# A hybrid transformer layer on one core: TensorE pinned to the source's order, first up weights split sooner, convolution steps at a later rank

## The chip, the cores and the metric

The kernel runs on one core of a Trainium2 chip. TensorE does the matrix products, VectorE (DVE), ScalarE (ACT) and GpSimd (POOL) work on rows, and SyncE (SP) issues most of the transfers. The metric is the device time of one execution in microseconds; lower is better.

## The reference

One layer over 2048 tokens of width 1024, in float32: a gated linear attention (GLA) mixer with a residual, a feed-forward network with a causal convolution of three taps and a residual, and a last normalization. Cut to what is computed:

```
h = rmsnorm(x, mix_norm_w)
q, k, v, r, glr = split(h @ w_in)                 # 512, 512, 1024, 1024, 16 columns
log_a = log_sigmoid(glr @ w_gate2 + b_gate) / 16   # one gate per token, head and key
g = cumsum(log_a within chunks of 64 tokens)
k_dec = k * exp(g_end - g)
for each chunk:                                    # 4 heads, keys of 128, values of 256
    state = state * exp(g_end) + k_dec.T @ v
    o = q @ state
x = x + (rms_normalize(o) * norm_w * silu(r)) @ w_out
h = rmsnorm(x, ffn_norm_w)
u = h @ w_up                                       # 1024 -> 5632
u = u[t] * cw[2] + b + u[t-2] * cw[0] + u[t-1] * cw[1]
gate, val = split(u)                               # 2816 each
x = x + (silu(gate) * val) @ w_down
out = rmsnorm(x, final_norm_w)
```

## The kernel before

**Products.** Each float32 product is three matmuls on halves: a value is split into a rounded part hi (a cast on ScalarE) and the rest lo (a subtraction on VectorE, `split`), and `mm3p` (L179 to L189) issues hi·lo, lo·hi, hi·hi (lines L184, L185, L186 of the profile). The large products are cut further into 2 x 2 blocks and computed as seven block products p1 to p7 on sums and differences of the blocks; one such block product with 512 columns is 4 x 3 = 12 matmuls.

**Stages.** First come passes over the rows of x: R (the gate r and the gates' rank-16 projection), A and B (k, q, v of two heads each, with the chunk scan laid between their products), then Y (out-projection). After R the gates are finished: for each tile of 128 tokens `sums` makes pd on TensorE (L639) and an Exp on ScalarE (L640), and `totals` transposes its result into pe (L631). In the scan, og (L763) is a normalized and gated row of outputs, which TensorE transposes into px (L771). In Y a finished row of x goes to `x1_done`: sum of squares on ScalarE (L224), variance on VectorE (L226), its root on GpSimd (L228), the scaled row on ScalarE (L831); `blocks` then transposes it (pt_d, L840).

The up stage (`phase_u`) runs a list of jobs (half s of the sequence, group g of weights, product o, column block f). For a job, `prep` splits the weight block (casts L193, subtractions L194, into uw; p5, p6, p7 need a sum or a difference on GpSimd first, L1274 to L1280), TensorE multiplies into the accumulators ua (p1, p6, p7, p4), uc (p5, p3) or ub (p2), ScalarE copies them (c, L1297 and L1411) and VectorE adds into u (L1406, L1414, L1424). A full u goes through `conv`: one tap and the bias on ScalarE (L1313), two taps on VectorE (L1315), Silu on ScalarE for the gate half (L1317); `gated` multiplies gate and value on VectorE (L1322), stores the product through SP's queue and forms sums on GpSimd (L1344). `new_u` takes one of three u buffers and copies two columns of halo on GpSimd (L1303). There are four t buffers. The down stage follows.

**What sets the order.** The source is written with a clock of its own: `adv` adds 0.227 us for each matmul of 512 columns, and `later_do(us, fn)` writes work at the place where that clock has gone on by so many us; `flush` and `need` write it at once. All engines, TensorE among them, then get their order from a list scheduler: by rank (the order of writing) among the instructions that it thinks ready. `high_priority(n)` moves the rank of what is written inside it n instructions earlier, or later for a negative n. So the order on an engine can differ from the source's. On each engine the instructions run in the order so found. Weight tiles of the up stage come from `w_pair` (four slots, WB, shared with the passes before) and, from the seventh job on, from three more (wx). In the last unit of Y (seven products, counted by i), the source starts `phase_u` at i = 3, which loads the first raw weights; the rest of it runs after Y.

Of the kernel before, what the change touches and what calls it, by code (L numbers as in the profile page):

```python
# [13 lines left out]
AF = mybir.ActivationFunctionType  # L14
ALU = mybir.AluOpType
# [10 lines left out]
def hybrid_kernel(  # L26
# [14 lines left out]
    w_down: bass.AP,  # L41
    out: bass.AP,
):
    nc = tc.nc
    x = x[0]
    out = out[0]
# [9 lines left out]
    NTT = S // P  # L56
# [13 lines left out]
    LEAD = 2  # L70
    NLY, NLE = 5.5, 9.0
    NLS = 8.0
    Y0, Y1, U0, U1 = 3.0, 2.8, 14.0, 11.0
    HLY = (1.5, 3.0)
    TB0, TB1, TB2, TB3 = 4.0, 10.0, 3.0, 2.2
# [9 lines left out]
    TS = 1024  # L85
# [70 lines left out]
    def later_do(us, fn):  # L156
        heapq.heappush(delayed, (clock["now"] + us, next(seq), fn))
# [51 lines left out]
    cw = cst.tile([P, 4, 2 * NF], F32, name="cw")  # L209
    halo = cst.tile([P, 2 * NF, 2], F32, name="halo")  # L210
# [614 lines left out]
    def x1_done(t, xt):  # L825
        if "p" not in yp:
            y_open()
        (nc.scalar if t + 2 >= NTT else nc.sync).dma_start(x1d[t], xt)
        rws = yp["p"].tile([P, D], F32, tag="rows", name=f"h2_{t}", bufs=2)
        rstd = rstd_of(xt, D, f"d{t}", rws, "a")  # L830
        nc.scalar.activation(rws, xt, AF.Identity, scale=rstd)  # L831
        later_do(NLY if t + 2 < NTT else NLE, lambda: blocks(t, rws))

    def blocks(tt, rws):
# [291 lines left out]
    def unit(ps_, j):  # L1126
        e, d = 2 * j, 2 * j + 1
        g = "AB".find(ps_)
        nxt = PS[PS.index(ps_) + 1:][:1]
        c1, c2 = slice(0, 512), slice(512, 1024)  # L1130
        add = nc.vector.tensor_add
        bank, keep = {}, {}

        def scan_slot(m):
            if ps_ == "Y" and j < 2:
                for fn, n in SLOTS_END.get(28 * j + m, ()):
                    fn(2 * NTT + n)
            if ps_ in "AB":
                for fn, n in SLOTS.get(m, ()):
                    fn(NTT * g + e + n)  # L1140

        if ps_ == "R":
            if j + 2 < NP:
                for t in (e + 4, d + 4):
                    xin[t] = load_xt(t)
            if j + 1 < NP:
                for n in range(4):
                    later_do(TSQ * (n + 1), squares)
                for i, t in enumerate((e + 2, d + 2)):
                    later_do(TX[i], lambda t=t: blocks_x(t))  # L1150

        def out(src, other, name, t_):
            t = out_tile(f"{name}_{ps_}_{j}")
            nc.vector.scalar_tensor_tensor(t, src, rs[:, t_:t_ + 1], other, op0=ALU.mult, op1=ALU.add)
            return t

        if j + 1 == NP and nxt:
            (load_w if nxt == "A" else load_made)(nxt, RB)
        if ps_ in "AB" and j in (2, 4):
            make_sums(nxt, j // 2 - 1)  # L1160
        for i, o in enumerate(PORD):
            need_w(ps_, o)
            prep_rows(limit(ps_, j, i))
            if ps_ == "Y" and j + 2 < NP and i == 3:
                for t in (e + 2, d + 2):
                    xin[t] = load_x(t, "x1")
            if ps_ == "Y" and j + 2 == NP and i == 1:
                for t in (e + 2, d + 2):
                    xin[t] = yp["p"].tile([P, D], F32, tag="x7", name=f"x1_{t}", bufs=2)
                    nc.sync.dma_start(xin[t], x[t * P:(t + 1) * P, :])  # L1170
            hh, hl = rows.pop((ps_, j, o))
            wh, wl = W[ps_, o]
            pairs = [((hh[:, k * P:(k + 1) * P], hl[:, k * P:(k + 1) * P]), (wh[:, k, :], wl[:, k, :])) for k in range(HK)]
            if o in ("p1", "p5", "p2"):
                a = bank[o] = mm_ps(f"m{o}_{ps_}_{j}")
                mm3p(a, pairs, mid=lambda k: scan_slot(4 * i + k))
            else:
                a = bank["p5" if o == "p3" else "p1"]
                mm3p(a, pairs, first=False, more=True, mid=lambda k: scan_slot(4 * i + k))
            if ps_ == "R":  # L1180
                gate_mm(j, o, hh, hl)
            if j + 1 == NP:
                if nxt:
                    if i == 0:
                        plan_w(nxt)
                else:
                    if i == 0:
                        need(*(f"h2p{jj}" for jj in range(PAIRS)))
                    load_op(0, o)
                    if i == 3:  # L1190
                        ux["u"] = phase_u()
                        next(ux["u"])
            if ps_ == "Y":
                while d not in xin:
                    heapq.heappop(wevents)[-1]()
                xe, xd = xin[e], xin[d]
                for xt, cs in {"p1": ((xe, c1),), "p5": ((xd, c2),), "p6": ((xd, c1),), "p2": ((xe, c1),),
                               "p7": ((xd, c2),), "p3": ((xd, c1),), "p4": ((xe, c2),)}[o]:
                    add(xt[:, cs], xt[:, cs], a)
                if o in ("p3", "p4"):  # L1200
                    t, xt = (e, xe) if o == "p4" else (d, xd)
                    held.append((t, xt))
                if j < 2:
                    scan_slot(4 * i + 4)
                while held and not scan:
                    x1_done(*held.pop(0))
                continue
            if o in ("p1", "p5", "p6"):
                keep[o] = cp_tile(f"c{o}_{ps_}_{j}")
                t_ = e if o == "p1" else d  # L1210
                nc.scalar.activation(keep[o], a, AF.Identity, scale=rs[:, t_:t_ + 1])
            elif o == "p2":
                o11 = out(a, keep["p1"], "o11", e)
            elif o == "p7":
                o22 = out(a, keep["p5"], "o22", d)
            elif o == "p3":
                o12 = out(a, keep["p6"], "o12", d)
            if ps_ == "R":
                if o == "p2":
                    nc.sync.dma_start(rd[e][0], o11)  # L1220
                elif o == "p7":
                    nc.sync.dma_start(rd[d][1], o22)
                elif o == "p3":
                    nc.sync.dma_start(rd[d][0], o12)
                elif o == "p4":
                    o21 = out_tile(f"o21_{ps_}_{j}")
                    nc.scalar.activation(o21, a, AF.Identity, scale=rs[:, e:e + 1])
                    nc.sync.dma_start(rd[e][1], o21)
            else:
                n = NTT * g + e  # L1230
                if o == "p2":
                    if j == 0 and g == 0:
                        scan_a()
                    scan[n] = {"g": g, "t": e, "e": scan_e(g, e), "kq": o11}
                elif o == "p7":
                    scan[n + 1] = {"g": g, "t": d, "v": scan_v(g, d, o22)}
                elif o == "p3":
                    if j == 0 and g == 0:
                        scan_b()
                    scan[n + 1].update(kq=o12, e=scan_e(g, d))  # L1240
                elif o == "p4":
                    scan[n]["v"] = scan_v(g, e, a, rs[:, e:e + 1])
                scan_slot(4 * i + 4)
# [10 lines left out]
    def phase_u():  # L1254
# [45 lines left out]
        def new_u(s, i, f):  # L1300
            c = f + i * NF
            u = pools["us"].tile([P, TS + P], F32, tag="u", name=f"u_{s}_{c}", bufs=3)
            upool["ins"] = nc.gpsimd.tensor_copy(u[:, 0:2], halo[:, c, :])  # L1303
            made["u", i, f] = u
            return tiles2(u[:, 2:2 + TS])

        def conv(s, i, f):
            c = f + i * NF
            u = made.pop(("u", i, f))
            if s + 1 < NS:  # L1310
                nc.gpsimd.tensor_copy(halo[:, c, :], u[:, TS:TS + 2])
            t = pools["us"].tile([P, TS], F32, tag="t", name=f"t_{s}_{c}", bufs=4)
            nc.scalar.activation(t, u[:, 2:2 + TS], AF.Identity, scale=cw[:, 2, c:c + 1], bias=cw[:, 3, c:c + 1])  # L1313
            for k in range(2):
                nc.vector.scalar_tensor_tensor(t, u[:, k:k + TS], cw[:, k, c:c + 1], t, op0=ALU.mult, op1=ALU.add)  # L1315
            if i == 0:
                nc.scalar.activation(t, t, AF.Silu)  # L1317
            made["t", i, f] = t

        def gated(s, f):  # L1320
            t, v = made.pop(("t", 0, f)), made.pop(("t", 1, f))
            nc.vector.tensor_mul(t, t, v)  # L1322
            q = f // 2
            made["a", f % 2] = even, odd = tiles2(t)

# [27 lines left out]
        load(0, 0)  # L1353
        load(0, 1)
        yield
        done = 0
        bank = {}
        for k, (s, g, o, f) in enumerate(jobs):
            if s == 1 and k % GJ in GATHER:
# [318 lines left out]
```

## Time and profile before

| what | value |
|---|---|
| median of 3 runs | 2109.62 us (2108.34 to 2113.0) |
| the profiled execution | 2105.53 us |
| its span | 2103.8 us, mean granted clock 0.994 |
| TensorE busy | 2048.0 us, 97% |
| VectorE busy | 1604.0 us, 76% |
| ScalarE busy | 1109.2 us, 53% |
| GpSimd busy | 667.9 us, 32% |

Times in the profile are microseconds from the start of the span unless marked ns. In the timeline a row is start, duration, engine, line, operation, output <- inputs, shape, count, and in brackets the idle time ahead of it with the work that ended it. In the waits a row is the engine and the work that waited, what it waited for, then us in total, times, and the longest. In the rows by stretch a row is the stretch and its length, then busy time (count) of PE, PEld (weight load), DVE, ACT and POOL, then TensorE's granted clock, DMA share and GB/s. The first product of the up stage begins at 820.00 us; the stage lasts to about 1710 us.

### The profile page before, as it was taken

The numbers are of one execution on the slowest core, as the hardware profiler recorded it, in microseconds if no ns is written. First come the engines' busy times: TensorE is split into PE (matmuls) and PEld (weight loads), VectorE is DVE, ScalarE is ACT, GpSimd is POOL, SyncE is SP. The second block draws the span as 40 slices with busy tenths as digits, with TensorE's granted clock in tenths as the row PEclk, the third lists the DMA queues.
The fourth block names the chain that finished last, engine by engine and source line by source line (L and its number), as shares of the span: only waits on it lengthen the run. The fifth ranks groups of instructions, "written<-read, shape, count | busy, mean of one in ns | idle before, by whom it ended". The sixth has DMA issues, their size and how long they took to land.

```text
span 2103.8 us, 28198 instructions
## 1 busy us (share of the span) xinstructions
PE 2048.0 (97%) x9700; PEld 1685.5 (80%) x9700; DVE 1604.0 (76%) x2109; ACT 1109.2 (53%) x2022; POOL 667.9 (32%) x595
## 2 busy tenths in 40 slices
PE   6999999999998998999999999999999999999998
PEld 5887788878886887888888887888888788888886
DVE  8766887887888556899898867898898956466464
ACT  5666755676565667545545444455454533223342
POOL 2110000000000003454553544666766432243210
PEclk9999999999999999999999999999999999999999
DMA  9876775577767977445445386545445684444462
GB/s 315 280 235 207 230 239 173 174 261 250 274 207 261 326 255 280 165 140 163 163 135 194 106 285 210 131 115 160 111 133 147 196 325 155 161 167 163 151 217 113
DMA packets 246512, 419.32 MB, mean 199 GB/s; under 512 B 22784, under 2 KB 91520, under 8 KB 246368
## 3 DMA queue, kind: packets, MB, share of 16 engines
q1 hardware_dynamic: 203200, 335.09, 46.9%
q10 hardware_dynamic: 36832, 70.89, 9.8%
q0 software_dynamic: 6336, 11.54, 3.5%
q8 instruction: 76, 1.25, 0.2%
q14 instruction: 68, 0.56, 0.1%
HBM read 278.50 MB, written 150.47 MB: 204 GB/s over the span
## 4 chain that ended last, share of the span: by engine, by line
PE 68%; DVE 11%; POOL 7%; issue 7%; DMA 6%; ACT 2%; SPq 0%; DVEq 0%; POOLq 0%; ACTq 0%
PE pd_p L186 7%; PE pd_p L185 7%; PE pd_p L184 7%; DVE t L1315 4%; PE ua L185 4%; PE ua L184 3%; PE ua L186 3%; DVE uw_p L194 3%; PE mp_A L184 2%; POOL as_p L1344 2%; PE mp_A L185 2%; PE mp_A L186 2%; PE mp_Y L185 2%; PE mp_Y L184 2%; PE mp_Y L186 2%
## 5 line engine op out<-in xcount | busy, mean ns | idle before, releaser
L184 PE MATMUL ua<-h_p,uw_p 128*128 128x512 f32 x704 | 276.4, 393 | 9.2 <-ACT c L1297 4.1
L185 PE MATMUL ua<-h_p,uw_p 128*128 128x512 f32 x704 | 275.3, 391 | 2.8 <-DVE var_d L226 2.8
L186 PE MATMUL ua<-h_p,uw_p 128*128 128x512 f32 x704 | 275.0, 391 | 0.0
L1315 DVE SCALAR_TENSOR_TENSOR t<-u,cw,t 128x1024 f32<-128x1024 f32 x176 | 258.4, 1471 | 6.3 <-ACT t L1313 5.6
L185 PE MATMUL pd_p<-dw_p,da 128*128 128x512 f32 x616 | 239.8, 389 | 0.0
L184 PE MATMUL pd_p<-dw_p,da 128*128 128x512 f32 x616 | 239.6, 389 | 0.0
L186 PE MATMUL pd_p<-dw_p,da 128*128 128x512 f32 x616 | 239.6, 389 | 0.0
L193 ACT CAST uw_p<-us 128x512 fp32r<-128x512 f32 x132 | 82.2, 622 | 196.1 <-POOL us L1277 127.2
L194 DVE TENSOR_TENSOR uw_p<-us,uw_p 128x512 fp32r<-128x512 f32 x132 | 153.2, 1165 | 42.0 <-ACT uw_p L193 40.6
L194 DVE TENSOR_TENSOR da<-da_p,da 128x512 fp32r<-128x512 f32 x154 | 117.9, 820 | 84.9 <-ACT da L193 84.9
L194 DVE TENSOR_TENSOR uw_p<-ur,uw_p 128x512 fp32r<-128x512 f32 x176 | 150.0, 880 | 27.4 <-ACT uw_p L193 27.2
L184 PEld LDWEIGHTS ua<-h_p,uw_p 128*128 128x128 f32 x704 | 132.5, 188 | 41.8 <-ACT c L1297 8.5
L193 ACT CAST da<-da_p 128x512 fp32r<-128x512 f32 x154 | 84.7, 618 | 146.1 <-PE pd_p L186 111.4
L185 PEld LDWEIGHTS ua<-h_p,uw_p 128*128 128x128 f32 x704 | 132.9, 189 | 30.6 <-DVE uw_p L194 3.3
L186 PEld LDWEIGHTS ua<-h_p,uw_p 128*128 128x128 f32 x704 | 132.7, 189 | 27.8
L760 POOL TENSOR_TENSOR rstd<-var,pair 128x2 f32<-128x2 f32 x32 | 22.7, 710 | 401.7 <-DVE var L759 401.7
L184 PE MATMUL uc<-h_p,uw_p 128*128 128x512 f32 x352 | 137.1, 389 | 1.2 <-DMA h_p<-hd_p 1.2
L185 PE MATMUL uc<-h_p,uw_p 128*128 128x512 f32 x352 | 136.9, 389 | 0.0
L186 PE MATMUL uc<-h_p,uw_p 128*128 128x512 f32 x352 | 136.9, 389 | 0.0
L1313 ACT ACTIVATE t<-u,cw 128x1024 f32<-128x1024 f32 x88 | 109.6, 1245 | 49.9 <-DVE u L1424 49.6
L185 PEld LDWEIGHTS pd_p<-dw_p,da 128*128 128x128 f32 x616 | 115.6, 188 | 24.5 <-DVE da L194 0.4
L186 PEld LDWEIGHTS pd_p<-dw_p,da 128*128 128x128 f32 x616 | 115.6, 188 | 24.0
(263 smaller groups left out, 5285.6 us busy)
## 6 DMA issues: line engine op xcount, KB each, us to landing
ur<-in_ffn_w_up_dram SPq DMA_DIRECT2D x84, 512.0 KB, 4.9
da_p<-ad_p SPq DMA_DIRECT2D x154, 256.0 KB, 4.2
ad_p<-t SPq DMA_DIRECT2D x110, 256.0 KB, 3.2
ch<-in_ffn_w_down_dram SPq DMA_DIRECT2D x61, 256.0 KB, 5.1
hr_A_p<-h1d_p SPq DMA_DIRECT2D x56, 256.0 KB, 3.1
hr_B_p<-h1d_p SPq DMA_DIRECT2D x56, 256.0 KB, 3.4
hr_Y_p<-yd_p SPq DMA_DIRECT2D x56, 256.0 KB, 3.7
hd_p<-h2p_p ACTq DMA_DIRECT2D x56, 256.0 KB, 2.0
```

Of the source, the lines that this page charges most:

```text
L184: nc.tensor.matmul(ps_ap, ah, bl, start=(first and i == 0), stop=False, **kw)
L185: nc.tensor.matmul(ps_ap, al, bh, start=False, stop=False, **kw)
L186: nc.tensor.matmul(ps_ap, ah, bh, start=False, stop=(last and i == len(pairs) - 1), **kw)
L193: order["act"] = nc.scalar.copy(hi, src)
L194: nc.vector.tensor_sub(lo, src, f32(hi))
L760: nc.gpsimd.tensor_tensor(rstd, var, neghalf.to_broadcast([P, 2]), op=ALU.pow)
L1313: nc.scalar.activation(t, u[:, 2:2 + TS], AF.Identity, scale=cw[:, 2, c:c + 1], bias=cw[:, 3, c:c + 1])
L1315: nc.vector.scalar_tensor_tensor(t, u[:, k:k + TS], cw[:, k, c:c + 1], t, op0=ALU.mult, op1=ALU.add)
L1344: upool["ins"] = nc.gpsimd.tensor_add(av, last if x is None else x, y)
```

## The change

TensorE is put under a manual schedule: it issues its instructions in the order in which the source writes them. The other engines stay with the scheduler. For the last two row tiles of Y, `x1_done` writes the scaled row (L831) 4 us of source clock later. `phase_u` is resumed at i = 3, 5 and 6 of the last Y unit instead of 3 alone, and at 5 and 6 it writes the weight splits of its first two jobs, ranked 200 earlier. In the up stage, the halo copy of `new_u` and the product of `gated` are ranked 120 later, and the two taps on VectorE and the Silu 80 later; the tap on ScalarE (L1313) stays.

```diff
+    ctx.enter_context(tc.manual_schedule(engines={mybir.EngineType.PE}))
     nc = tc.nc
...
     NLS = 8.0
+    NLX = 4.0
...
         rstd = rstd_of(xt, D, f"d{t}", rws, "a")
-        nc.scalar.activation(rws, xt, AF.Identity, scale=rstd)
+
+        def scaled():
+            nc.scalar.activation(rws, xt, AF.Identity, scale=rstd)
+
+        if t + 2 < NTT:
+            scaled()
+        else:
+            later_do(NLX, scaled)
         later_do(NLY if t + 2 < NTT else NLE, lambda: blocks(t, rws))
...
                     if i == 3:
                         ux["u"] = phase_u()
+                    if i in (3, 5, 6):
                         next(ux["u"])
...
             u = pools["us"].tile([P, TS + P], F32, tag="u", name=f"u_{s}_{c}", bufs=3)
-            upool["ins"] = nc.gpsimd.tensor_copy(u[:, 0:2], halo[:, c, :])
+            with tc.high_priority(-120):
+                upool["ins"] = nc.gpsimd.tensor_copy(u[:, 0:2], halo[:, c, :])
...
             nc.scalar.activation(t, u[:, 2:2 + TS], AF.Identity, scale=cw[:, 2, c:c + 1], bias=cw[:, 3, c:c + 1])
-            for k in range(2):
-                nc.vector.scalar_tensor_tensor(t, u[:, k:k + TS], cw[:, k, c:c + 1], t, op0=ALU.mult, op1=ALU.add)
-            if i == 0:
-                nc.scalar.activation(t, t, AF.Silu)
+            with tc.high_priority(-80):
+                for k in range(2):
+                    nc.vector.scalar_tensor_tensor(t, u[:, k:k + TS], cw[:, k, c:c + 1], t, op0=ALU.mult, op1=ALU.add)
+                if i == 0:
+                    nc.scalar.activation(t, t, AF.Silu)
...
-            nc.vector.tensor_mul(t, t, v)
+            with tc.high_priority(-120):
+                nc.vector.tensor_mul(t, t, v)
...
         load(0, 1)
         yield
-        done = 0
+        for done in range(1, 3):
+            with tc.high_priority(200):
+                prep(done - 1)
+            yield
```

## The prediction

> **What bounds the kernel now.** I read the head of the page first, then the engines, then the waits of TensorE over the whole span.
>
> ```profile
> span 2103.8 us, 28198 instructions
> PE 2048.0 (97%) x9700; PEld 1685.5 (80%) x9700; DVE 1604.0 (76%) x2109; ACT 1109.2 (53%) x2022; POOL 667.9 (32%) x595
> PE m_R L184 <- DVE w_R_p L194: 12.5, 3, 9.8
> PE ua L184 <- ACT c L1297: 4.1, 6, 1.2
> PE ua L184 <- ACT uw_p L193: 3.1, 1, 3.1
> PE ua L185 <- DVE var_d L226: 2.8, 1, 2.8
> PE ua L184 <- ACT c L1411: 2.0, 1, 2.0
> ```
>
> TensorE computes in 2048.0 of 2103.8 us, and the change takes no matmul away. So the change can only trade among 2103.8 − 2048.0 = 55.8 us of idle time, and in the half-clock time that sits inside the busy 2048.0. The waits (us in all, times, longest) say where the idle time lies. The largest, 12.5 us, is the wait for the first weights of the kernel, which nothing here touches. The change aims at the lines with ua: 3.1 + 2.8 us at the start of the up stage, 4.1 us inside it. Next I cut the span by stage (the stretch, PE busy, PEld, DVE, ACT, POOL, then the granted clock).
>
> ```profile
> 820.00:850.00 30.00, 27.19 (x115) 21.84 (x116) 21.04 (x26) 24.16 (x47) 12.45 (x11) 0.89 0.55 209
> 824.00:829.00 5.00, 5.00 (x13) 3.95 (x14) 1.27 (x3) 3.72 (x5) 1.97 (x3) 0.54 0.95 376
> 850.00:1710.00 860.00, 852.74 (x3748) 702.02 (x3748) 741.33 (x720) 436.72 (x658) 477.98 (x384) 1.00 0.53 163
> ```
>
> The up stage proper (850 to 1710) holds only 860 − 852.74 = 7.3 us of idle TensorE, and VectorE is next at 741 of 860: there is little to win, and the second engine has room. The start of the up stage is worse than its waits say: after them TensorE runs at 0.54 of its clock. One matmul follows the other in 852.74/3748 = 0.2275 us there. The down stage after 1710 has none of the edited code.
>
> **Part 1, first weights split sooner.** Here are TensorE, then ScalarE, then VectorE around the start of the up stage.
>
> ```profile
> 816.56 0.39 PE L186 MATMUL mp_Y<-w_Y_p,h_Y_p 128*128 128x512 f32 x1
> 820.00 1.02 PE L184 MATMUL ua<-h_p,uw_p 128*128 128x512 f32 x2 [3.06 <-ACT uw_p L193]
> 823.81 0.80 PE L185 MATMUL ua<-h_p,uw_p 128*128 128x512 f32 x1 [2.79 <-DVE var_d L226]
> 831.16 0.39 PE L184 MATMUL uc<-h_p,uw_p 128*128 128x512 f32 x1
> 819.34 1.14 ACT L193 CAST uw_p<-ur 128x512 fp32r<-128x512 f32 x2
> 824.86 1.15 ACT L831 ACTIVATE h<-x,rstd_d 128x1024 f32<-128x1024 f32 x1 [3.34 <-POOL rstd_d L228]
> 826.96 0.60 ACT L193 CAST uw_p<-us 128x512 fp32r<-128x512 f32 x1
> 818.65 3.91 DVE L194 TENSOR_TENSOR h_p<-h_p 128x1024 fp32r<-128x1024 f32 x2
> 822.48 0.68 DVE L1199 TENSOR_TENSOR x<-x,mp_Y 128x512 f32<-128x512 f32 x1
> 823.08 0.68 DVE L194 TENSOR_TENSOR uw_p<-ur,uw_p 128x512 fp32r<-128x512 f32 x1
> 827.64 0.69 DVE L194 TENSOR_TENSOR uw_p<-us,uw_p 128x512 fp32r<-128x512 f32 x1 [0.34 <-ACT uw_p L193]
> ```
>
> Out-projection ends at 816.8 (816.56 plus one spacing of 0.23). The first up product p1 waits for the rounded weight (cast at 819.34), then for its rest on VectorE (823.08; the row calls the releaser var_d, a 0.14-us neighbour of it). The first p5 product (uc) begins at 831.16. Between lie 24 matmuls of p1 (two products of 4 x 3), which are 24 x 0.227 = 5.5 us; so 831.16 − 816.8 − 5.5 = 8.9 us are lost: that is the most this part can give.
>
> The two casts and two subtractions move ahead by up to 4 us; their count does not change. The slots that they write are those of the last Y unit's p2 and p7 weights, read for the last time before 812, so no slot holds them. If both are there at 816.8, p1 runs to 816.8 + 5.5 = 822.3. What is late next is the p5 weight: its subtraction stands at 827.64, behind a cast at 826.96, which stands on ScalarE behind the scaled row of L831, which waited 3.34 us for rstd_d. The change puts that L831 4 us later on the source clock, so the cast can go when its sum on GpSimd is there (about 820). The subtraction is then held by VectorE alone, which has no break from 818.65 to 823.76. Its work there is the same in another order, so the p5 rest comes at about 823.8 + 0.7 = 824.5, and uc at 824.7. Gain 831.16 − 824.7 = 6.5; a half-clock spell after the 2.4 us wait would take up to 1.7 back (priced below). **I take −6.0**, ends −8.9 (no wait) and −3 (L831 still ahead of the cast: uc at 828.3). The later L831 feeds rows which are read only in the second half of the up stage; that cover is hundreds of us. Two early subtractions (1.2 us) also stand ahead of the last Y product's row on VectorE; at most 0.6 us of Y waits for them, inside the ends.
>
> **Part 2, convolution at a later rank.** The waits for the copy c (L1297) look alike; the Silu ahead of one of them, and all of another, on ScalarE:
>
> ```profile
> 880.72 1.06 ACT L1317 ACTIVATE t<-t 128x1024 f32<-128x1024 f32 x1 [2.07 <-DVE t L1315]
> 1336.36 1.25 ACT L1313 ACTIVATE t<-u,cw 128x1024 f32<-128x1024 f32 x1 [1.45 <-DVE u L1424]
> 1337.99 1.06 ACT L1317 ACTIVATE t<-t 128x1024 f32<-128x1024 f32 x1 [0.38 <-DVE t L1315]
> 1338.95 0.57 ACT L1297 COPY c<-ua 128x512 f32<-128x512 f32 x1
> 1658.53 0.62 ACT L193 CAST da<-da_p 128x512 fp32r<-128x512 f32 x1 [0.61 <-DMA da_p<-ad_p]
> ```
>
> ScalarE stands in its queue at the Silu (L1317), which waits for VectorE's convolution step; behind it stands the copy that frees TensorE's accumulator. With the Silu ranked 80 later the copies pass it. The steps moved are 176 on VectorE, 44 Silu, 44 products of gated and 88 halo copies on GpSimd; behind gated hang the stores of t on SP's queue and GpSimd's additions, which the down stage reads much later. Their count is unchanged, so the worth is the six waits: 4.1 us plus six restarts of about 0.15 us (816.79 and the wait of 3.06 make 819.85, and ua begins at 820.00), 5.0 in all. L1313, not moved, still stands ahead of some copies (1336.36), and the 2.0 us at L1411 came with a cast that waited for a transfer (1658.53), which no rank here moves. **I take −4.5**, ends −7 (the L1411 wait goes too) and +4. The loss would come if later steps free the three u buffers too late: then u's addition, and with it the accumulators, would wait (GpSimd's halo copy, 120 later, opens each u); VectorE's 741 of 860 leaves about 119 us of room over 44 products, 2.7 us for each, so I lean to the gain.
>
> **Part 3, TensorE in source order.** Nothing is added, but 532 of 9700 matmuls leave their present places, in 21 places: where the scheduler had slipped main products ahead of a small product whose input was late, TensorE now stands. The costliest is the end of the gates (231 to 249), where the source lists pe of tile 12, pd, pe of 13, pd, pe of 14, pd, pe of 15 with no mp_A between. Each pe needs the Exp of the pd before it (TensorE, then ScalarE):
>
> ```profile
> 233.43 0.66 PE L631 MATMUL pe<-ident,e 128*128 128x128 f32 x4
> 235.80 0.39 PE L639 MATMUL pd<-ll,later 128*128 128x512 f32 x1
> 237.18 0.60 PE L631 MATMUL pe<-ident,e 128*128 128x128 f32 x4
> 241.53 0.66 PE L631 MATMUL pe<-ident,e 128*128 128x128 f32 x4
> 243.88 0.60 PE L631 MATMUL pe<-ident,e 128*128 128x128 f32 x4
> 239.59 1.28 ACT L640 ACT_TABLE_LOAD   x1
> ```
>
> At today's times TensorE would stand from 233.9 to 235.5, 236.3 to 237.2, 238.1 to 241.5 and 242.4 to 243.9: 1.6 + 0.9 + 3.4 + 1.5 = 7.4 us, now filled by mp_A matmuls. With less of mp_A's work between, ScalarE has less reason to switch to Silu and back (two table loads like that at 239.59, 2 x 1.28 = 2.6): **+4.8**, ends 0 (the chain closes up and later waits go instead) and 7.4. The other places, by the nearest rows:
>
> ```profile
> 648.09 0.90 PE L771 MATMUL px<-ident,og 128*128 128x128 f32 x3 [4.27 <-DVE og L763]
> 634.86 0.41 PE L771 MATMUL px<-ident,og 128*128 128x128 f32 x2 [0.93 <-DVE og L763]
> 648.65 0.78 PE L184 MATMUL mp_Y<-w_Y_p,h_Y_p 128*128 128x512 f32 x1
> 422.35 0.41 PE L771 MATMUL px<-ident,og 128*128 128x128 f32 x2
> 425.89 0.50 PE L185 MATMUL mp_B<-w_B_p,h_B_p 128*128 128x512 f32 x1 [1.79 <-DVE h_B_p L194]
> PE mp_B L184 <- ACT cp_B L1211: 1.9, 2, 1.1
> 32.97 0.57 PE L184 MATMUL m_R<-w_R_p,h_R 128*128 128x512 f32 x1 [2.13 <-DVE w_R_p L194]
> 33.00:41.00 8.00, 7.32 (x24) 5.52 (x24) 5.35 (x8) 2.74 (x8) 4.79 (x3) 0.79 0.93 326
> ```
>
> A stall has a second price, the clock. After 2.13 us of idle time at 32.97 the clock is 0.79 over 8 us: 8 x 0.21 = 1.7 us more. After 4.27 us at 648.09 the next mp_Y took 0.78 us instead of 0.39. After 1.79 us at 425.89 it took 0.50 and no more. So I charge 1.7 us for each spell over 2 us.
>
> At the start of pass B the source has a px 13 matmuls earlier, so it would wait 13 x 0.23 = 3.0 us longer; those matmuls then fill the 1.79 us and part of the 1.9 us for cp_B: net +0.5, and a spell over 2 us: +2.2. At the end of the scan the px at 634.86 stands ahead of 12 mp_Y matmuls, 2.7 us more; those fill 2.7 of the 4.27 us later, which leaves 1.6 and so gives back one half-clock spell while a new one comes (0.93 + 2.7 = 3.6 us): between −1.7 and +2.7, taken as −1.5, as the spells here are close enough together to share one. The rest are single waits of about a microsecond; those ahead of 820 run into the wait there: 0. Of the gates' four, 1.6, 0.9 and 1.5 are under 2 us and the 3.4 less the loads is 0.8: no charge. **Pinning: 4.8 + 2.2 − 1.5 = +5.5**, ends +1 (gates and start of B closed up) and +15.
>
> The Trainium skill's page "TensorE: Matmul & The Clock Gate" (section "Why this matters for your kernels") asks only that no gap of TensorE exceed about 3 us. By that rule the 3.0 and 3.6 us would just about halve the clock and the 2.13 would not; the trace's 2.13 us did, so I keep the row.
>
> **Sum.** −6.0 − 4.5 + 5.5 = −5.0. Against the profiled execution (2105.53 us, its span 2103.8 plus 1.7) that is 2100.5. The median of the three runs, 2109.62, stands 4.1 above that execution; in its frame 2104.6 us, −0.24%. What a measurement of this kernel tells from no change is 0.2%, 4.2 us, so this forecast lies barely outside.
>
> **The rivals.**
> - Full gain: the gates close up (0), the p5 weight is there in time (−8.9), the copies all pass (−5.0): −13.9, 2095.7. For it: every wait named has its cause in the edited rows. Against: VectorE has no break before 823.76.
> - It doesn't do what it says: the p5 weight stays behind L831 (−3), the copies stay behind L1313 or other late work (−1), pinning costs 3.5: −0.5, 2109.1. For it: 1336.36, where L1313 itself waits.
> - Slower, the pinned spells stay whole, each with its half clock: gates 7.4 + two spells of 1.7 = 10.8, start of B 3.0 − 1.8 + 1.7 = 2.9, end of scan 2.7 + 1.7 = 4.4: 18.1 instead of 5.5; less 10.5 gives +7.6, 2117.2. It decides from 10.5 us of pinning cost on (slower by over 0.2% from 14.7). For it: 32.97 and the row after it, and the table loads. Against: the displaced main matmuls fill later waits.
> - The same waits with the clock held through them: 18.1 less four spells of 1.7 is 11.3, less 10.5 gives +0.8, 2110.4. Against: the same two rows. By the page's rule named above, spells just under 3 us would end like this.
>
> **How the numbers follow.** Likeliest sum 0.43 (own range 2101 to 2108, two thirds of it beyond −0.2%), full gain 0.17, no effect 0.17, slower 0.18, clock held 0.05. Faster: 0.29 + 0.17 + 0.02 = 0.48; slower: 0.17 of its 0.18, 0.03 from no effect, 0.01 from the held clock: 0.21; the same: the rest, 0.31. The range takes the full gain and about half of the slower case: 2094 to 2117.
>
> **What the profile of the changed kernel would show.** Part 1: the ua rows from about 817 at 0.23 us spacing, the waits of 3.1 and 2.8 gone, one wait of some 2.4 us at the first uc; right if uc begins 5 to 8 us earlier relative to the end of mp_Y. Part 2: the line ua from c L1297 under 1 us; PE busy over 856 of the 860 us like 850 to 1710; wrong if new waits for u's additions (uc or ub after DVE) stand there. Part 3: pe from e L640 as a wait of several us between 231 and 249, px from og near 419 and 631; PE's clock row shows whether half-clock spells follow. The prediction fails high if those spells are many, and low if the main products in source order also remove waits which I counted as fixed in the passes before 820.

## The result, and the profile after

The changed kernel takes 2125.18 us (median of 5 runs, 2122.17 to 2130.03) against 2108.34 us (5 runs, 2106.16 to 2113.0): a ratio of 1.0076 with an interval of 1.0059 to 1.0094. It is 0.76%, about 16 us, slower, where 0.24% faster was forecast, and it lies above the range of 2094 to 2117. The profiled execution took 2122.17 us; its page begins:

```profile
span 2120.5 us, 28201 instructions
PE 2051.4 (97%) x9700; PEld 1693.4 (80%) x9700; DVE 1588.7 (75%) x2109; ACT 1114.2 (53%) x2024; POOL 676.9 (32%) x595
```

Both kernels issue the same 9700 matmuls, so the stages can be compared by count: the time from the start of one matmul to the start of another, counted in order of issue. The first column runs from the start of the span to number 1000 (pass R), the next to 1200 (end of the gates), 3200 (A and most of B), 4000 (end of the scan, Y), 4400 (start of the up stage), 8000 (up stage) and the end. The other rows are the profiled executions of the experiments below; us throughout.

| kernel | R | gates | A, B | scan end, Y | start of up | up | down | span |
|---|---|---|---|---|---|---|---|---|
| before | 208.7 | 44.2 | 363.2 | 170.5 | 97.7 | 825.3 | 394.1 | 2103.8 |
| after | 210.7 | 57.0 | 362.9 | 174.8 | 97.7 | 823.2 | 394.3 | 2120.5 |
| pin only | 209.4 | 55.9 | 365.7 | 175.1 | 98.8 | 824.8 | 393.9 | 2123.6 |
| no pin | 209.3 | 44.2 | 365.5 | 170.4 | 94.0 | 823.6 | 395.6 | 2102.6 |
| gates' flush free | 209.9 | 48.1 | 365.7 | 175.3 | 98.3 | 821.7 | 394.4 | 2113.4 |
| no Silu there | 210.7 | 50.9 | 365.2 | 173.4 | 98.3 | 822.3 | 393.9 | 2114.7 |
| gates earlier | 209.1 | 49.6 | 366.8 | 176.1 | 97.7 | 822.0 | 394.9 | 2116.2 |
| pin after gates | 210.1 | 49.2 | 369.2 | 175.2 | 98.3 | 822.6 | 395.9 | 2120.5 |
| pin from up on | 210.4 | 44.2 | 363.4 | 172.3 | 96.4 | 821.7 | 394.0 | 2102.6 |
| pin from job 7 on | 210.2 | 44.2 | 364.3 | 169.5 | 94.0 | 821.7 | 393.9 | 2097.9 |
| later transposes | 208.9 | 44.2 | 364.4 | 168.6 | 104.2 | 822.3 | 394.6 | 2107.3 |
| ranks only | 210.8 | 44.2 | 362.9 | 171.7 | 96.3 | 822.2 | 394.6 | 2102.8 |
| splits only | 210.7 | 44.2 | 363.0 | 171.8 | 95.5 | 823.8 | 394.6 | 2103.6 |

In kernels whose passes are not pinned the columns vary from one execution to another by 2 to 4 us (R 208.7 to 210.8, A and B 362.9 to 365.5, Y 168.6 to 172.3), so one such difference says little. The gates' column is steady, 44.2 in all of them. Of the 16.7 us that the span grew, 12.8 are there, 4.3 at the end of the scan and in Y (a column that varies by 3.7 by itself); the up stage gives 2.1 back; its start gives nothing.

Some of TensorE's waits over the whole span of the changed kernel (us, times, longest; its line numbers stand 2 to 16 later than before's):

```profile
PE px L773 <- DVE og L765: 8.2, 3, 3.6
PE pe L633 <- ACT e L642: 6.8, 3, 3.3
PE mp_Y L186 <- DVE x L1209: 5.1, 1, 5.1
PE pt_d L849 <- ACT h L835: 4.3, 4, 2.0
PE mp_A L186 <- ACT cp_A L1221: 3.8, 3, 2.7
PE ua L186 <- ACT c L1307: 2.0, 1, 2.0
PE uc L186 <- DMA h_p<-hd_p: 2.0, 1, 2.0
PE ub L186 <- DMA h_p<-hd_p: 1.3, 1, 1.3
```

The waits that the change aimed at are gone or halved (ua from uw_p, 3.1, and from var_d, 2.8, have no row; ua from c 4.1 to 2.0). In their place stand small products that now hold the main ones back: pe from e (1.0 before), px from og (5.5 before), pt_d from h (0.2 before). The gates' end in the changed kernel, TensorE first and then ScalarE:

```profile
224.40 0.79 PE L186 MATMUL mp_A<-w_A_p,h_A_p 128*128 128x512 f32 x1 [2.69 <-ACT cp_A L1221]
239.14 0.50 PE L641 MATMUL pd<-ll,later 128*128 128x512 f32 x1 [1.82 <-DVE ll L196]
245.21 0.66 PE L633 MATMUL pe<-ident,e 128*128 128x128 f32 x4 [2.37 <-ACT e L642]
249.62 1.12 PE L633 MATMUL pe<-ident,e 128*128 128x128 f32 x4 [3.29 <-ACT e L642]
241.26 1.28 ACT L716 ACT_TABLE_LOAD   x1
243.26 1.28 ACT L642 ACT_TABLE_LOAD   x1
244.56 0.60 ACT L642 ACTIVATE e<-pd 128x512 f32<-128x512 f32 x1
245.68 1.28 ACT L716 ACT_TABLE_LOAD   x1
247.67 1.28 ACT L642 ACT_TABLE_LOAD   x1
248.97 0.60 ACT L642 ACTIVATE e<-pd 128x512 f32<-128x512 f32 x1
```

Each of the last two Exps comes after a switch to the Silu's table (L716) and back: in ScalarE's order, which the scheduler still makes, a Silu stands between these Exps, where the next pd is not there yet. TensorE stands through both switches. Before and after by slices (the granted clock follows the entry of POOL); before comes first, with its one long wait near the first place:

```profile
221.37 0.50 PE L185 MATMUL mp_A<-w_A_p,h_A_p 128*128 128x512 f32 x1 [1.39 <-DVE h_A_p L194]
224.50:228.00 3.50, 3.36 (x16) 2.46 (x15) 2.71 (x5) 3.50 (x7) 0.00 (x0) 1.00 0.68 185
244.00:248.00 4.00, 4.00 (x23) 3.16 (x21) 1.65 (x4) 3.98 (x9) 0.00 (x0) 1.00 0.64 159
```

```profile
224.50:228.00 3.50, 3.50 (x9) 2.73 (x10) 3.07 (x4) 2.86 (x6) 0.00 (x0) 0.50 0.82 266
228.00:232.00 4.00, 4.00 (x14) 3.15 (x13) 2.61 (x3) 3.03 (x6) 0.00 (x0) 0.68 0.45 152
248.00:252.00 4.00, 2.38 (x8) 2.09 (x9) 0.37 (x1) 2.12 (x4) 0.00 (x0) 0.50 0.74 241
252.00:256.00 4.00, 4.00 (x15) 3.14 (x14) 0.54 (x2) 0.69 (x2) 0.00 (x0) 0.69 0.47 159
```

Busy time at a lowered clock costs 3.5 x 0.5 + 4 x 0.32 = 3.0 us after the first wait and 2.38 x 0.5 + 4 x 0.31 = 2.4 after the last. The four waits make 10.2 us; before, a wait of 1.4 us (for h_A_p, not for cp_A) stood near the first place. Together 10.2 − 1.4 + 5.4 = 14 us, near the 12.8 of the table.

### The profile page after: what moved, and what is told of

Its sections match the earlier page's. It is cut to its first block, busy times and chain, and to the rows that moved or that the text cites. A ratio compares the mean times of both kernels' runs of the same rounds, so it can differ in the third digit from the quotient of the medians.

```text
span 2120.5 us, 28201 instructions
## 1 busy us (share of the span) xinstructions
PE 2051.4 (97%) x9700; PEld 1693.4 (80%) x9700; DVE 1588.7 (75%) x2109; ACT 1114.2 (53%) x2024; POOL 676.9 (32%) x595
## 4 chain that ended last, share of the span: by engine, by line
PE 66%; DVE 10%; POOL 8%; issue 7%; DMA 4%; ACT 3%; SPq 1%; ACTq 0%; POOLq 0%; DVEq 0%
PE pd_p L187 7%; PE pd_p L188 7%; PE pd_p L186 7%; PE ua L186 3%; PE ua L187 3%; PE ua L188 3%; POOL as_p L1357 3%; DVE t L1327 3%; DVE uw_p L196 3%; PE mp_A L186 2%; PE mp_A L188 2%; PE mp_A L187 2%; PE mp_Y L186 2%; PE mp_Y L187 2%; PE mp_Y L188 2%
## 5 line engine op out<-in xcount | busy, mean ns | idle before, releaser
L196 DVE TENSOR_TENSOR uw_p<-us,uw_p 128x512 fp32r<-128x512 f32 x132 | 145.8, 1105 | 40.1 <-ACT uw_p L195 40.0
```

The lines of the kernel that those rows point to most:

```text
L196: nc.vector.tensor_sub(lo, src, f32(hi))
```

## The experiments

Two theories stood against each other. Theory 1: the pin alone makes the loss, mostly at the gates. The rival: the pin costs about what was forecast, and the splits or the ranks do harm. All ratios below are to the kernel before on the same chip, five rounds each.

**Pin only.** Edit, on the kernel before:

```diff
+    ctx.enter_context(tc.manual_schedule(engines={mybir.EngineType.PE}))
```

> The kernel before with TensorE pinned to the source's order and nothing else of the change. Theory 1 (the pin alone makes the loss: its waits at the end of the gates, and the half clock after them): before + 16 to 19 us, 0.8 to 0.9% slower, with about 13 us of it between 200 and 253 us. Rival (the pin costs the 5.5 us that were forecast and the rest comes with the early splits or the later ranks): before + 4 to 8 us.

Measured: 2126.89 us, ratio 1.0092 (1.0072 to 1.0113), 19 us slower (15 to 24), with 11.7 us of it in the gates' column. By the medians the pin alone costs about 3 us more than the whole change, though the two intervals overlap. The rival falls.

**No pin.** Edit, on the changed kernel:

```diff
-    ctx.enter_context(tc.manual_schedule(engines={mybir.EngineType.PE}))
```

> The changed kernel without the pin; early splits and later ranks stay. Theory 1: what is left can only help, 2 to 8 us faster than before (0.1 to 0.4%), and the gates between 200 and 253 us look as before. Rival (the early splits or the ranks cost something themselves): 5 us or more slower than before.

Measured: 2103.35 us, ratio 0.9973 (0.9960 to 0.9985), about 6 us faster than before; gates 44.2, start of up 3.7 us shorter. The rest of the change does help, and without the pin nothing of the loss is left.

**The gates' flush free.** Edit, on the changed kernel (the pin is lifted while `need` writes the gates' last steps):

```diff
+        pin["ctx"].close()
         need(*(f"gates{t}" for t in range(NTT)))
+        pin_on()
```

> The changed kernel with the pin lifted for the writing of the gates' last steps alone (the pd and pe that are written in one go ahead of the scan), so that the scheduler may lay main products between them. Theory 1 (the order of these steps is the main cost): 11 to 13 us less than the changed kernel, 2112 to 2114 in the frame of 2125. Rival (the cost is spread over all pinned places, or ScalarE's own order makes it): 4 us less or fewer.

Measured: 2115.11 us, ratio 1.0035 (1.0023 to 1.0048): 9 to 10 us less than the changed kernel, short of the 11 to 13. The gates' column falls by 8.9; the first wait there, for cp_A, stays (2.72 us), since it lies ahead of the edit.

**No Silu there.** Edit, on the changed kernel:

```diff
-        nc.scalar.activation(r, r, AF.Silu)
+        nc.scalar.activation(r, r, AF.Silu if n > 2 else AF.Identity)
```

> The changed kernel, whole pin, with the Silu of the first three tiles of r replaced by a plain copy (those rows of the gate are left without their Silu), so that ScalarE has no reason to change its table between the Exps of the last gates. Theory 1 (in the pinned chain each Exp pays for a switch to Silu and back): the waits of TensorE for e fall by about 2.6 us each at two places, and one half-clock spell of 1.7 goes: 4 to 7 us less than the changed kernel. Rival (the chain from pd over Exp to pe is slow by itself): under 1.5 us less.

Measured: 2116.38 us, ratio 1.0034 (1.0021 to 1.0048), about 9 us less than the changed kernel by the two ratios, more than the 4 to 7 expected; the gates' column itself falls by 6.1, inside them. The two waits for e:

```profile
243.89 0.66 PE L633 MATMUL pe<-ident,e 128*128 128x128 f32 x4 [0.81 <-ACT e L642]
245.71 0.66 PE L633 MATMUL pe<-ident,e 128*128 128x128 f32 x4 [0.69 <-ACT e L642]
248.00:252.00 4.00, 4.00 (x20) 3.24 (x20) 0.61 (x1) 1.36 (x3) 0.00 (x0) 1.00 1.04 375
```

2.37 and 3.29 became 0.81 and 0.69, 4.2 us less, and between 248 and 252 us the clock is at 1.00 where it was 0.50. A slow spell is left, though: 0.81 and 0.77 from 236 to 244 us, where it had been 1.00. And about 1.3 us of the 6.1 is only a shorter slow clock after the wait for cp_A, ahead of these Silus (last section). So a third of the gates' loss, the 4.2 us of waits, is shown to be the price of the table switches, which main products had covered; how much slow clock to add is not settled by one execution.

**Gates earlier.** Edit, on the changed kernel:

```diff
-            gates(j // 2, TB0, TB1, TB2)
+            gates(j // 2, TB0, TB1 if j < 7 else 5.0, TB2)
```

> The changed kernel, whole pin, with the last gates' steps written 5 us of source clock earlier, so that main products stand between most of them in the source too. Theory 1 (the pin costs because the source writes these steps in one go): the gates' part between 208 and 255 us loses 7 to 10 us instead of 17.8; 7 to 11 us less than the changed kernel. Rival (the inputs of these steps come too late wherever they are written, so TensorE waits for each at its new place): under 4 us less.

Measured: 2118.5 us, ratio 1.0046 (1.0033 to 1.0060), 6 us less than the changed kernel. The gates' column falls by 7.4. The writing in one go is a cause; the 7 to 11 us that were expected are just missed by the median, and the column of A and B is 3.9 us longer in this execution than in the changed kernel's.

**Pin after the gates.** Edit, on the changed kernel: no pin at the start, and at the gates' end

```diff
         need(*(f"gates{t}" for t in range(NTT)))
+        pin_on()
```

> The changed kernel with the pin from just after the gates on (passes A, B, Y, up, down). Theory 1 (outside the gates the pin costs little: 2 us at the end of the scan, 1 to 3 in Y and A, paid back by the later part): 12 to 15 us less than the changed kernel, 2110 to 2113 in the frame of 2125, still 2 to 5 us slower than before. Rival (the pin costs nothing outside the gates): the same as with the pin from the up stage on, 4 to 6 us faster than before.

Measured: 2119.75 us, ratio 1.0046 (1.0031 to 1.0061), 6 us less than the changed kernel; 12 to 15 were expected. That expectation was wrong in two places. The gates still take 49.2 (the wait for cp_A is gone, 1.39 for h_A_p as before): TensorE waits for an e although these steps are not pinned:

```profile
242.90 0.66 PE L638 MATMUL pe<-ident,e 128*128 128x128 f32 x4 [2.83 <-ACT e L647]
```

Only the main products behind them are tied to one another there; why fewer of them pass was not tried. And the columns of A, B and of Y lie 5.8 and 2.9 us above those of the pin from the up stage on (the line below it in the table), in an execution some 2.5 us above the median. By the ratios the two kernels lie 14.7 us apart, and the gates' columns explain 5.0 of it. So the pin has a second price in the passes with the scan, and theory 1, which gave these passes only a few us, is wrong.

**Pin from the up stage on.** Edit, on the changed kernel:

```diff
+    pin_on()
     for _ in ux["u"]:
```

> The changed kernel with the pin from the end of the last Y unit on alone (up stage and down stage). Theory 1: the passes cost what they did before; the start of the up stage gives nothing, because transposes of the last rows (pt_d) wait in TensorE's order where the early splits had saved 6.7 us; the rest of the up stage saves about 2 us: 0 to 3 us faster than before. Rival (the pin in the up stage is what makes the early splits pay): 6 to 9 us faster than before.

Measured: 2102.23 us, ratio 0.9976 (0.9966 to 0.9985), 5 us faster than before, between the two expectations. The start of up gains 1.3, the up stage 3.6; the latter need not be the pin's, since the ranks alone, without any pin, show 3.1 there (822.2).

**Pin from the seventh job on.** Edit: `pin_on()` stands after the last delayed work is written at job 7 (k == 6) instead.

> The changed kernel with the pin from the seventh job of the up stage on alone, after the last transposes pt_d. Theory 1 (the start keeps the 3.8 us that it gains without the pin, and the pinned rest of the up stage the 3.6 us that it gained with it): 6.5 to 8 us faster than before, 0.31 to 0.38%. Rival (the pinned rest only gave back what the pinned start had lost): 4 to 5 us faster, as with the pin from the start of the up stage.

Measured: 2100.73 us, ratio 0.9973 (0.9963 to 0.9983). The columns are as theory 1 has them (94.0 and 821.7, which is 7.3 us less than before), but the ratio says 5.7 us, short of the 6.5 to 8, and its interval holds the 0.9976 of the pin from the up stage on. This is the lowest median of all, and faster than both kernels; against no pin at all (0.9973) it is a draw.

**Later transposes.** Edit, on the pin from the up stage on:

```diff
-    NLY, NLE = 5.5, 9.0
+    NLY, NLE = 5.5, 15.0
```

> The changed kernel with the pin from the end of the last Y unit on, and the transposes pt_d of the last two row tiles written 15 us of source clock after their rows instead of 9. Theory 1 (TensorE waited there only because these transposes stood too early in its order): the 2.1 and 0.6 us of waits for pt_d go, 7 to 8 us faster than before. Rival (another wait takes their place, such as for the p5 weight's rest): 4 to 5 us faster, as with 9 us.

Measured: 2112.75 us, ratio 1.0024 (1.0011 to 1.0037), slower than before: worse than either theory. The waits for pt_d are gone, as theory 1 had it, but the start of up is 104.2. TensorE, then ScalarE, in that run:

```profile
851.77 0.80 PE L191 MATMUL ua<-h_p,uw_p 128*128 128x512 f32 x1 [7.67 <-ACT c L1312]
843.28 1.14 ACT L858 ACTIVATE hb<-pt_d,nw 128x128 f32<-128x128 f32 x4 [0.74 <-DMA h2f<-hb]
847.95 1.14 ACT L858 ACTIVATE hb<-pt_d,nw 128x128 f32<-128x128 f32 x4 [1.97 <-DMA h2f<-hb]
851.13 0.59 ACT L1312 COPY c<-ua 128x512 f32<-128x512 f32 x1 [2.04 <-DMA h2f<-hb]
```

The rows hb and the copies c share the four tiles of `cp_tile`. Written later, the rows fall among the copies, and rows and copies wait for a store of hb to free a tile; the copy c stands behind the rows in ScalarE's queue, waits 2.04 us for a tile itself, and TensorE's accumulator waits for c.

**Ranks only**, the three `high_priority` edits of the up stage on the kernel before:

> The kernel before with the later ranks alone. Theory 1 (the ranks take away waits for the copy c, and bring new waits for transfers of h_p): 1 to 2.5 us faster than before; between 850 and 1710 us TensorE loses 4 to 5 us where it lost 6.3. Rival (the ranks are worth the 4.5 us that were forecast): 4 to 5 us faster.

Measured: 2103.97 us, ratio 0.9986 (0.9975 to 0.9996), 3 us faster, between the two expectations. Some waits between 850 and 1710 us:

```profile
PE ua L184 <- ACT c L1297: 2.0, 1, 2.0
PE uc L184 <- DMA h_p<-hd_p: 1.9, 1, 1.9
PE ub L184 <- DMA h_p<-hd_p: 0.6, 1, 0.6
```

The copies still cost 2.0 instead of 4.1, and the wait for h_p, 1.2 before, is now 2.5 in two places (uc and ub). The second place, ub, shows in all kernels with the ranks and in none without them; what in the ranks delays the transfer was not tried.

**Splits only**, the edits of `x1_done` and `prep` on the kernel before:

> The kernel before with the early weight splits and the later scaled row alone, no pin and no ranks. Theory 1 (without the pin the transposes pt_d move out of the way, and the start keeps most of the gain): 3 to 5 us faster than before. Rival (the splits are worth nothing, and the gain seen without the pin came from the ranks): within 1 us of before.

Measured: 2104.4 us, ratio 0.9992 (0.9978 to 1.0006): 2 us faster at most likely, not clear of no change and short of the 3 to 5 expected. In its trace the start of up is 2.2 us shorter than before (1.4 shorter with the ranks only, so part of it may be chance).

## Why the prediction was wrong, point by point

**Part 3, the pin: the term that failed.** Forecast +5.5, ends +1 and +15; measured alone +19 (15 to 24 by the interval). The rival "the pinned spells stay whole, each with its half clock" had 18.1 and was given 0.18. It comes near the 19 in sum, in part by luck: it had no wait for cp_A, and its 2.9 at the start of B is not seen in the column of A and B (−0.3). Four steps of the forecast went wrong:
- The gates' +4.8 took two table loads off because ScalarE would have "less reason to switch". It switched there and back twice, once more than before; without the Silu the same waits are 4.2 us shorter. The chain did not close up, because ScalarE's order, which is not pinned, now has a Silu in each of the last two gaps between Exps.
- Of the four waits reckoned there (1.6, 0.9, 3.4 and 1.5, in all 7.4 us) the third was cut to 0.8. Measured are 1.82, none, 2.37 and 3.29, in all 7.5: the uncut sum was right. No half clock was charged, and after the last wait the clock was at 0.50, which cost 2.4 us.
- Counting the "single waits of about a microsecond" at 0 left out the wait for cp_A at 224.40. The copy stands in ScalarE's queue behind two Softplus steps (row below). TensorE waits 2.7 us for it in every kernel that is pinned there, and 1.4 us for h_A_p instead in every kernel that is not. In the changed kernel 3.0 us of slow clock followed.
- At the end of the scan the displaced products were to fill the later 4.27 us, taken as −1.5. The 4.27 came back as 5.14 under another name. The rows for the last two points and for the start of B (436.89), ScalarE's first:

```profile
222.62 1.15 ACT L622 ACTIVATE e<-e 128x512 f32<-128x512 f32 x2
223.68 0.67 ACT L1221 ACTIVATE cp_A<-mp_A,rs 128x512 f32<-128x512 f32 x1
436.89 0.74 PE L773 MATMUL px<-ident,og 128*128 128x128 f32 x4 [3.12 <-DVE og L765]
647.97 1.09 PE L773 MATMUL px<-ident,og 128*128 128x128 f32 x4 [3.57 <-DVE og L765]
664.72 0.77 PE L186 MATMUL mp_Y<-w_Y_p,h_Y_p 128*128 128x512 f32 x1 [5.14 <-DVE x L1209]
```

The px wait forecast as 3.6 is 3.57, and a later mp_Y then waits 5.14 us for an accumulator. Here a wait was moved, not filled; that rests on the trace, as no run frees these steps alone. At the start of B the wait came as forecast (3.12 for 3.0), but the half clock charged with it did not: the clock behind it was 1.00 (last section), and the column of A and B did not rise.

**Part 1, the splits: right in its steps, lost behind them.** The two waits went, p1 ran without a break, and the first wait at uc is the p5 weight's rest:

```profile
836.72 0.39 PE L186 MATMUL ua<-h_p,uw_p 128*128 128x512 f32 x1
842.16 0.39 PE L186 MATMUL uc<-h_p,uw_p 128*128 128x512 f32 x1
844.40 0.50 PE L187 MATMUL uc<-h_p,uw_p 128*128 128x512 f32 x1 [1.85 <-DVE var_d L228]
847.21 1.15 ACT L835 ACTIVATE h<-x,rstd_d 128x1024 f32<-128x1024 f32 x1 [1.91 <-POOL rstd_d L230]
848.41 1.97 PE L849 MATMUL pt_d<-ident,h 128*128 128x128 f32 x8 [1.98 <-ACT h L835]
855.33 0.66 PE L849 MATMUL pt_d<-ident,h 128*128 128x128 f32 x4 [1.48 <-ACT hb L853]
```

The second uc matmul stands 7.7 us after the start of ua; the forecast had 7.9. But the stage did not get shorter (97.7 both): after six uc matmuls TensorE stands for pt_d, whose place in the source lies in the middle of uc and whose row is scaled later now. That row waits for its root (1.91 us), which stands on GpSimd behind a sum of weights (L1287, 844.42 to 846.67), so the later writing of the row is not shown to be what held it. The clock is low from the first of these waits on:

```profile
844.00:848.00 4.00, 2.03 (x5) 1.13 (x5) 1.60 (x4) 1.94 (x3) 3.27 (x3) 0.62 1.02 408
848.00:852.00 4.00, 3.59 (x13) 3.24 (x14) 1.92 (x2) 4.00 (x6) 0.50 (x1) 0.53 0.17 68
```

TensorE's waits here make 5.9 us (the three shown and one of 0.63), the slow clock 2.03 x 0.38 + 3.59 x 0.47 = 2.5: 8.4 us, about the 8.9 that were lost before. The prediction said that the scaled row feeds only the second half of the stage; it overlooked that the transposes of that row stand in TensorE's pinned order. Unpinned they slide, and the start is 2 to 4 us shorter (splits only, no pin). So −6.0 was too large even there, because later weights' rests on VectorE bring waits of 0.4 to 1.2 us in turn.

**Part 2, the ranks: right sign, less by the median.** Forecast −4.5, measured −3 alone (−1 to −5), which does not exclude the forecast. One wait for c (2.0 us, where under 1 was expected) and a longer wait for h_p stayed; the waits for u's additions that would have made it a loss did not come.

**Sum.** By parts measured alone: +19 − 3 − 2 = +14, against +16 for the whole; the two do not differ beyond their intervals.

## What to carry to other kernels

Pinning an engine to the source makes every late small operation in the source's order a stop for all that follows, so the source must be written for that first. If you pin at all, pin a region that has no such chains, and let the scheduler keep the rest; here no pinned kernel beat the one without the pin by its ratio. When you price a forced order, take the waits whole, add a range for the slow clock behind each (none to 3.0 us here), and do not count on the other engines to close the chain up: their order may put something else into the gap. A wait that ends earlier on one engine is only a gain if the next operation in the engine's order is not waiting too.

## What the runs showed of the hardware

The slow clock after a wait does not have one length, and the length of the wait alone does not decide it. After 2.69 us of idle time at 224.40 the clock was 0.50 to 228 and 0.68 to 232, 3.0 us lost; in the run without the Silu the wait there was as long (2.66), and the clock was 0.54 and then 0.97:

```profile
224.39 0.49 PE L186 MATMUL mp_A<-w_A_p,h_A_p 128*128 128x512 f32 x1 [2.66 <-ACT cp_A L1221]
224.50:228.00 3.50, 3.50 (x9) 2.73 (x10) 3.05 (x4) 2.87 (x6) 0.00 (x0) 0.54 0.80 270
228.00:232.00 4.00, 4.00 (x19) 3.29 (x18) 2.87 (x4) 3.93 (x5) 0.00 (x0) 0.97 0.48 151
```

That is 3.5 x 0.46 + 4 x 0.03 = 1.7 us. The forecast's flat 1.7 us for a spell (1.5 if only the 7.32 busy of its 8 us are counted) can thus be exceeded. It can also be missed altogether: in the changed kernel the clock stayed at 1.00 after the px wait of 3.12 us (436.89), while the same wait with the pin alone left it at 0.75 there (the changed kernel first):

```profile
437.00:441.00 4.00, 4.00 (x21) 3.29 (x22) 3.96 (x8) 3.11 (x6) 0.00 (x0) 1.00 0.67 224
437.00:441.00 4.00, 4.00 (x17) 3.31 (x16) 3.98 (x6) 2.71 (x5) 0.00 (x0) 0.75 0.63 220
```

The Trainium skill's page "TensorE: Matmul & The Clock Gate" (section "Why this matters for your kernels") asks for no gap over about 3 us. These traces differ from that rule both ways: after 1.85 us at 844.40 the clock was 0.62, after 3.12 us at 436.89 it was 1.00.
